# The first mixer's softmax attention, projected first and traced between the other tiles

## The chip, the cores and the metric

The kernel runs on one core of a Trainium2 chip. The metric is the device time of one execution in microseconds (us). Before the change it is 2632.47 us, the median of three runs (2630.48 to 2641.77). All views of the profile below come from one further execution, taken by the hardware profiler.

## The reference

The reference is a stack of four residual layers on 256 context and 256 latent tokens of width 1024; each layer is a mixer followed by a feed-forward network. The change concerns the first mixer only:

```python
h = jnp.concatenate([h_ctx, h_lat], axis=1)                  # 512 tokens x 1024
gq, gk, gv, gog, gz, aq, ak, av = _split(h @ w_in, EVEN_SIZES)
# linear attention, 4 heads: gated recurrence in both directions, norm per head, times silu(gog)
g = _heads(jax.nn.log_sigmoid(logit) / GLA_GATE_TAU, GLA_HEADS)
a_lat = _gated_readout(dirs[0][1] + dirs[1][1], og[:, :, n_ctx:], gla_out_norm)
# softmax attention, 8 query heads on 2 key heads: RMS norm per head, rotary on the latent tokens;
# context queries see the context keys, latent queries see all keys
qa = _rms(aq..., att_q_norm); ka = _rms(ak..., att_k_norm)
b_ctx = _softmax_attend(qa[:, :, :, :n_ctx], ka[:, :, :n_ctx], va[:, :, :n_ctx])
o = jnp.concatenate([a, b], axis=-1)                         # then o @ w_out
```

Everything is computed in float32 accuracy: a projection splits both operands into a high and a low part of type fp32r and adds three products; the attention itself uses plain fp32.

## The kernel before, in words

The text is Python that traces instructions for five engines. A planner then orders them: each instruction has its place in the trace as its priority, an engine takes what is ready and stands first, and a tile waits until one of its `bufs` buffers is free. So a stream that is traced between two pieces of work is offered to the engines there, and a stream that is traced behind them fills gaps. On the chip each engine runs its instructions strictly in the planned order.

The first mixer is `even_mixer`. It first makes the values and the gate's input, `linear_tm` on `ew_tm`, and from these the decay factors `ga` (L545 to L559). Then come 13 projection tiles of 128 output columns, `linear_steps` on `ew_fm` (L591): a 512 KB weight tile is loaded by SP's queue (four `raw` buffers), split by ScalarE and VectorE (L194, L195), and multiplied with all 512 tokens by 24 matmuls in one of the three PSUM banks tagged `pl` (L204 to L206; the first three tiles in two halves). `consume` (L569) takes each result out of PSUM. The order of the tiles is K, Q, K, Q of the linear attention (tiles 0 to 3), the keys and four query tiles of the softmax attention (4 to 8), and four output gates (9 to 12, Silu). For the softmax tiles, `consume` also squares the tile and sums the squares per head and token on TensorE into the bank `ss` (L583).

Two streams follow. `gla` (L610), one for each of two pairs of heads, is the linear attention: seven levels, each with eight fp32 matmuls (sixteen records) in the two `pa` banks, a copy of keys on ScalarE, two masked copies and two products on VectorE; then the products across 128 and 256 tokens; then for each head the product with V, the norm per token (`rstd_rows`, a chain of eleven small VectorE steps), its broadcast by TensorE, and `readout` (L699): VectorE, GpSimd, ScalarE and VectorE in turn write rows 0 to 3 of `M`. `gqa` (L707) is the softmax attention: it makes the norm's factors from `ss`, applies them to the keys, does the rotary products of keys and queries, and then runs 16 units (4 query tiles, 2 key heads, 2 segments of tokens). `attend` (L943) traces the scores and the softmax of a unit (`attend_s`: scores in a `pl` bank, maximum, Exp on ScalarE, reciprocal, scaling) and then the value product of the unit before (`attend_v`: transposes into a `pl` bank, a copy, products into a `pb` bank). After four units `put_hl` (L1013) writes a row of `M` (4 to 7) from the `pb` bank.

`M` takes the two buffers tagged `X` that hold the mixer's input, so it can be allocated only behind the last projection tile. The trace before is: four tiles; then nine tiles, with one step of the two `gla` streams after each; then `M`; then the rest of `gla` and the whole of `gqa` in turn, step by step (L591 to L600). The output projection (`ew_out`) reads the rows of `M` in the order 0 to 7.

Of the kernel before, what the change touches and what calls it, by code (L numbers as in the profile page):

```python
# [8 lines left out]
F32 = mybir.dt.float32  # L9
# [35 lines left out]
def in_turn(streams):  # L45

    streams = list(streams)
    while streams:
        for g in list(streams):
            if next(g, True) is None:  # L50
                yield
            else:
                streams.remove(g)
# [74 lines left out]
class Kern:  # L128
# [396 lines left out]
    def even_mixer(self, X, mix, pre, sc):  # L525
        nc, A = self.nc, self.A
        mm = nc.tensor.matmul
        self.load_masks(mix)
        self.s5_powers(mix, sc)
        V = mix.tile([P, 4, 672], F32, tag="V", name="V0")  # L530

        def put(c, tt, ps):
            nc.scalar.copy(V[:, tt, c * 336:(c + 1) * 336], ps)

        self.linear_tm(A["ew_tm"], X, 4, put, pre=pre)

        zp = self.psum("pa")
        for tt in range(4):
            mm(zp[:32, tt * P:(tt + 1) * P], V[:, tt, 640:672], self.ident, start=True, stop=True)
        z = mix.tile([32, 512], F32, tag="KC", name="z", bufs=2)  # L540
        nc.vector.tensor_copy(z, zp[:32, :])
        wg = mix.tile([32, 2, 256], F32, tag="KC", name="wg", bufs=2)
        nc.sync.dma_start(wg, A["gla_wg"])
        bg = self.gla_bg
        ga = []  # L545
        for t in range(2):
            a = mix.tile([P, 2, 512], F32, tag="g4", name=self.n("gla_a"), bufs=8)
            ab = mix.tile([P, 2, 512], F32, tag="g4", name=self.n("gla_ab"), bufs=8)
            for d in range(2):
                lp = self.psum("pa")  # L550
                mm(lp, wg[:, d, t * P:(t + 1) * P], z, start=True, stop=True)
                nc.scalar.activation(ab[:, d, :], lp, AF.Abs, bias=bg[:, d, t:t + 1])
                nc.vector.tensor_scalar(a[:, d, :], lp, bg[:, d, t:t + 1], 0.0, ALU.add, ALU.min)
            nc.scalar.activation(ab, ab, AF.Exp, scale=-1.0)
            nc.scalar.activation(ab, ab, AF.Ln, bias=1.0)
            nc.vector.tensor_tensor(a, a, ab, ALU.subtract)
            nc.scalar.activation(a, a, AF.Exp, scale=1.0 / 16.0)
            self.dbg(f"gla_a{t}", a)
            ga.append(a)  # L559
        K2 = [mix.tile([P, 2, 512], F32, tag="g4", name=self.n("K2"), bufs=8) for _ in range(2)]  # L560
        Q2 = [mix.tile([P, 2, 512], F32, tag="g4", name=self.n("Q2"), bufs=8) for _ in range(2)]
        qd = [mix.tile([P, 512], F32, tag="qd", name=self.n("qd"), bufs=2) for _ in range(2)]
        sog = mix.tile([P, 4, 512], F32, tag="sog", name="sog")
        qa = mix.tile([P, 4, 512], F32, tag="qa", name="qa")
        kg = mix.tile([P, 512], F32, tag="kg", name="kg")
        ss = self.psum("pb")
        gains = self.even_gains

        def consume(i, ps, *_):  # L569
            if i in (0, 2):  # L570
                nc.scalar.copy(K2[i // 2][:, 0, :], ps)
                nc.vector.tensor_copy(K2[i // 2][:, 1, :], ps)
            elif i in (1, 3):
                t = i // 2
                nc.scalar.mul(qd[t], ps, 0.25)
                for d in range(2):
                    nc.vector.scalar_tensor_tensor(Q2[t][:, d, :], ps, 0.125, ga[t][:, d, :], ALU.mult, ALU.mult)
            elif i < 9:
                sq = self.sm.tile([P, 512], F32, tag="sq", name=self.n("sq"), bufs=2)
                nc.scalar.activation(sq, ps, AF.Square)  # L580
                j = 8 if i == 4 else 2 * (i - 5)
                for tt in range(4):
                    mm(ss[:, 10 * tt + j:10 * tt + j + 2], sq[:, tt * P:(tt + 1) * P], self.hsel, start=True, stop=True)  # L583
                if i == 4:
                    nc.scalar.activation(kg, ps, AF.Identity, scale=gains[:, 1:2])
                else:
                    nc.scalar.activation(qa[:, i - 5, :], ps, AF.Identity, scale=gains[:, 0:1])
            else:
                nc.scalar.activation(sog[:, i - 9, :], ps, AF.Silu)

        tiles = self.linear_steps(A["ew_fm"], X, 512, consume)  # L591
        for _ in range(4):
            next(tiles)
        M = []
        gla = in_turn([self.gla(t, ga[t], K2[t], Q2[t], qd[t], V, sog, gains, M, mix) for t in range(2)])
        for _ in tiles:
            next(gla)
        M += [self.Xp.tile([P, KT, 512], F32R, tag="X", name=self.n("M")) for _ in range(2)]
        for _ in in_turn([gla, self.gqa(qa, kg, ss, V, M, mix)]):
            pass  # L600
        return M

# [104 lines left out]
    def gqa(self, qa, kg, ss, V, M, mix):  # L707
        nc, A = self.nc, self.A
        mm = nc.tensor.matmul
        r = self.sm.tile([P, 4, 10], F32, tag="rs40", name=self.n("rs"), bufs=2)  # L710
        self.rstd_rows(ss[:, :40], 64, 40, r.rearrange("p t h -> p (t h)"))
        rq = self.sm.tile([P, 4, 10], F32, tag="rs40", name=self.n("rq"), bufs=2)
        nc.vector.tensor_scalar(rq, r, 0.125, None, ALU.mult)
        bc = self.psum("pb")
        for h in range(2):
            for tt in range(4):
                mm(bc[64 * h:64 * h + 64, tt * P:(tt + 1) * P], r[:, tt, 8 + h:9 + h].to_broadcast([P, 64]),
                   self.ident, start=True, stop=True, skip_group_check=True)
        nc.vector.tensor_tensor(kg, kg, bc, ALU.mult)
        kz = [mix.tile([P, 512], F32, tag=f"kz{h}", name=self.n("kz")) for h in range(2)]  # L720
        cs = mix.tile([P, 2, 256], F32, tag="rope", name=self.n("rope"))
        nc.sync.dma_start(cs, A["rope0"])

        def rope(x, outs):
            sw = self.psum("pb")
            mm(sw[:, :256], self.perm32, x, start=True, stop=True)
            t = self.sm.tile([P, 512], F32, tag="nt", name=self.n("nt"), bufs=3)
            nc.vector.tensor_tensor(t[:, :256], sw[:, :256], cs[:, 1], ALU.mult)
            nc.vector.tensor_tensor(x, x, cs[:, 0], ALU.mult)
            for o, rs in outs:  # L730
                nc.vector.tensor_tensor(o[rs], x[rs], t[rs, :256], ALU.add)

        for h in range(2):
            rs = slice(64 * h, 64 * h + 64)
            nc.gpsimd.memset(kz[h][64 - 64 * h:128 - 64 * h, :], 0.0)
            nc.gpsimd.tensor_copy(kz[h][rs, :256], kg[rs, :256])
        rope(kg[:, 256:512], [(kz[h][:, 256:512], slice(64 * h, 64 * h + 64)) for h in range(2)])
        for t in range(4):
            rope(qa[:, t, 256:512], [(qa[:, t, 256:512], slice(0, P))])
        yield  # L740

        def units():
            for t in range(4):
                yield from self.pair_units(
                    [(qa[:, t], kz[h], V, slice(512 + 64 * h, 576 + 64 * h),
                      lambda tt, t=t, h=h: rq[:, tt, 2 * t + h:2 * t + h + 1]) for h in range(2)],
                    lambda po, t=t: self.put_hl(po, M, 4 + t))

        yield from self.attend(units(), mix)


# [98 lines left out]
    def hgrn_pair(self, p, al, ac, Kl, Kc, Q2, q, V, sog, gain, mix):  # L850
# [82 lines left out]
        for h in range(2):  # L933
            bc = self.psum(tag)
            for tt in range(2):
                mm(bc[:, tt * P:(tt + 1) * P], r[:, tt * 2 + h:tt * 2 + h + 1].to_broadcast([P, P]), self.ident,
                   start=True, stop=True)
            hd = 2 * p + h
            nc.vector.tensor_tensor(oS[h], oS[h], bc[:, :256], ALU.mult)
            nc.gpsimd.tensor_tensor(sog[:, hd], oS[h], sog[:, hd], ALU.mult)  # L940


    def attend(self, units, mix):  # L943
# [998 lines left out]
def prep(i):  # L1942
# [16 lines left out]
    for p in range(P):  # L1959
# [15 lines left out]
    A["ew_tm"] = np.ascontiguousarray(W[:, tm].reshape(4, 2, P, 2, 336).transpose(3, 0, 2, 1, 4))  # L1975
    aq = np.concatenate([1568 + 64 * h + hd for t in range(4) for h in (t, 4 + t)])
    ak = np.concatenate([2080 + 64 * h + hd for h in range(2)])
    A["ew_fm"] = _tiles(W, np.concatenate([np.arange(256, 384), np.arange(0, 128), np.arange(384, 512), np.arange(128, 256), ak, aq,
                                             np.arange(1024, 1536)]))
    rows = np.concatenate([np.arange(512)] + [512 + 64 * h + np.arange(64) for t in range(4) for h in (t, 4 + t)])  # L1980
    A["ew_out"] = _tiles(i["even_w_out"][0], rows=rows)
    wg = np.zeros((32, 2, 256), f)
# [118 lines left out]
```

## Time and profile before

| | |
|---|---|
| profiled execution | 2632.62 us |
| its span, first to last instruction | 2630.8 us |
| mean granted TensorE clock | 0.954 of full |
| TensorE (PE) matmuls busy | 2420.2 us (92%) |
| VectorE (DVE) busy | 1695.3 us (64%) |
| ScalarE (ACT) busy | 982.1 us (37%) |
| GpSimd (POOL) busy | 503.9 us (19%) |

A busy TensorE is not one at its peak, since its matmuls are pipelined and their ends are modelled. Where matmuls follow each other without a wait, the time from one start to the next is what one of them costs. PEld is TensorE's loading of weights. Times within the trace count from the span's first instruction. The 13 projection tiles run from about 97 to 233 us, and the mixer's last row of `M` is written at 353 us.

### The profile page before, as it was taken

The page shows a single profiled execution, that of the slowest core. Times are in us where ns is not written, and L with a number is a line of the kernel's source. Part 1 is how long each engine was busy: PE and PEld are TensorE (multiplying, and loading weights), DVE is VectorE, ACT ScalarE, POOL GpSimd, SP SyncE. Part 2 cuts the span into 40 slices and gives each one's busy share as a digit, 9 for nine tenths or more (in the row PEclk, how much of TensorE's full clock was granted, in tenths as well). Part 3 has the DMA queues.
Part 4 walks back from the last instruction along what each step waited for, and adds up shares of the span by engine and source line. Part 5 has one row for each costly group of instructions (what it writes and reads, how often), then busy time and mean ns, then how long its engine had stood idle before and what let it go on. Part 6 is the DMA issues. An engine that isn't in the chain of part 4 may idle for free.

```text
span 2630.8 us, 40272 instructions
## 1 busy us (share of the span) xinstructions
PE 2420.2 (92%) x15525; PEld 1974.6 (75%) x15525; DVE 1695.3 (64%) x3417; ACT 982.1 (37%) x1597; POOL 503.9 (19%) x648
## 2 busy tenths in 40 slices
PE   6999998889889988889899999999999999959999
PEld 3567676667678777889699888456787989628999
DVE  4336646998987488975455642665588744485666
ACT  4423424222223253333444443444433223435443
POOL 1810014652720033230100100110100000170000
PEclk9898998999999988999999999999999999989999
DMA  8741032676766234411675532001365533876454
GB/s 270 246 142 41 1 125 74 192 208 189 203 198 194 86 122 142 129 49 65 248 238 182 188 99 88 25 17 35 130 185 183 166 112 97 159 269 231 154 180 152
DMA packets 173294, 382.23 MB, mean 145 GB/s; under 512 B 25296, under 2 KB 71248, under 8 KB 172976
## 3 DMA queue, kind: packets, MB, share of 16 engines
q1 hardware_dynamic: 170096, 372.46, 45.0%
q0 software_dynamic: 3008, 7.21, 1.0%
q8 instruction: 122, 2.00, 0.3%
q14 instruction: 68, 0.56, 0.1%
HBM read 348.94 MB, written 30.67 MB: 144 GB/s over the span
## 4 chain that ended last, share of the span: by engine, by line
PE 46%; DVE 18%; DMA 9%; issue 5%; ACT 3%; POOL 0%; DVEq 0%; SPq 0%; ACTq 0%; POOLq 0%
PE pl L204 11%; PE pl L205 11%; PE pl L206 11%; DVE pm L374 5%; DMA mcol<-ada_t 3%; DVE lo L195 3%; DMA mcol<-mod_t 3%; DMA mrow<-crow 2%; PE pa L76 1%; DVE Wt L1435 1%; PE pa L880 1%; PE pl L963 1%; PE pa L994 1%; PE pm L1267 1%; PE pm L310 1%
## 5 line engine op out<-in xcount | busy, mean ns | idle before, releaser
L194 ACT CAST hi<-raw 128x1024 fp32r<-128x1024 f32 (+4 forms) x393 | 400.2, 1019 | 807.3 <-PE pl L205 610.5
L195 DVE TENSOR_TENSOR lo<-raw,hi 128x1024 fp32r<-128x1024 f32 (+4 forms) x393 | 486.3, 1239 | 315.8 <-ACT hi L194 314.5
L205 PE MATMUL pl<-X,hi 128*128 128x256 f32 (+1 forms) x2032 | 655.3, 324 | 7.4 <-POOL X L469 6.5
L204 PE MATMUL pl<-X,hi 128*128 128x256 f32 (+1 forms) x2032 | 658.9, 326 | 1.9 <-ACT X L466 1.9
L206 PE MATMUL pl<-X,lo 128*128 128x256 f32 (+1 forms) x2032 | 653.9, 323 | 7.2 <-DVE lo L195 7.2
L205 PEld LDWEIGHTS pl<-X,hi 128*128 128x128 f32 x2032 | 397.8, 196 | 45.3 <-issue 9.8
L206 PEld LDWEIGHTS pl<-X,lo 128*128 128x128 f32 x2032 | 397.6, 196 | 42.6 <-DVE lo L195 9.1
L204 PEld LDWEIGHTS pl<-X,hi 128*128 128x128 f32 x2032 | 397.0, 196 | 40.4 <-issue 12.5
L374 DVE SCALAR_TENSOR_TENSOR pm<-mcol,mrow 128x512 f32<-128x512 f32 x384 | 309.4, 806 | 82.7 <-DMA mcol<-ada_t 33.7
L204 PE MATMUL pl<-hh,hi 128*128 128x256 f32 (+1 forms) x1071 | 330.4, 310 | 11.9 <-ACT hh L1673 11.8
L205 PE MATMUL pl<-hl,hi 128*128 128x256 f32 (+1 forms) x1071 | 329.2, 308 | 6.3 <-DVE hl L1674 6.2
L206 PE MATMUL pl<-hh,lo 128*128 128x256 f32 (+1 forms) x1071 | 327.9, 307 | 0.0
L204 PEld LDWEIGHTS pl<-hh,hi 128*128 128x128 f32 x1071 | 204.1, 191 | 33.3 <-ACT hh L1673 13.4
L205 PEld LDWEIGHTS pl<-hl,hi 128*128 128x128 f32 x1071 | 204.8, 191 | 18.9 <-DVE hl L1674 8.4
L206 PEld LDWEIGHTS pl<-hh,lo 128*128 128x128 f32 x1071 | 204.9, 191 | 10.2 <-issue 0.4
L204 PE MATMUL pl<-M,hi 128*128 128x256 f32 (+1 forms) x416 | 124.1, 301 | 0.9 <-ACT M L1016 0.6
L1450 POOL TENSOR_TENSOR Ec<-PGr,bc 128x576 f32<-128x576 f32 x64 | 100.3, 1577 | 127.5 <-PE pb L1458 64.4
L205 PE MATMUL pl<-M,hi 128*128 128x256 f32 (+1 forms) x416 | 121.8, 294 | 0.2 <-DVE M L835 0.2
L206 PE MATMUL pl<-M,lo 128*128 128x256 f32 (+1 forms) x416 | 121.0, 292 | 0.8 <-DVE lo L195 0.8
L1673 ACT CAST hh<-sg 128x512 fp32r<-128x512 f32 (+1 forms) x108 | 55.2, 512 | 175.3 <-DVE sg L1670 110.0
L1687 DVE TENSOR_TENSOR y<-y,pl 128x256 f32<-128x256 f32 (+1 forms) x86 | 45.2, 525 | 107.5 <-PE pl L206 107.0
L469 POOL TENSOR_TENSOR X<-nt,X 128x256 fp32r<-128x256 f32 x48 | 37.7, 785 | 378.5 <-ACT nt L468 378.5
(517 smaller groups left out, 3801.2 us busy)
## 6 DMA issues: line engine op xcount, KB each, us to landing
raw<-f_u SPq DMA_DIRECT2D x88, 512.0 KB, 3.6
raw<-p_u SPq DMA_DIRECT2D x64, 512.0 KB, 3.5
raw<-p_d SPq DMA_DIRECT2D x64, 512.0 KB, 3.6
mraw<-mod_w SPq DMA_DIRECT2D x48, 512.0 KB, 5.2
mcol<-mod_t SPq DMA_DIRECT2D x96, 256.0 KB, 3.1
mcol<-ada_t SPq DMA_DIRECT2D x96, 256.0 KB, 2.9
mraw<-ada_w SPq DMA_DIRECT2D x48, 512.0 KB, 6.8
raw<-ow_fm SPq DMA_DIRECT2D x32, 512.0 KB, 3.3
```

Source lines behind the costliest of these rows:

```text
L76: K.nc.tensor.matmul(self.ps[32 * j:32 * j + 32, :N], K.ones[:rows, :32], self.sq[:rows, :N], start=k < 4, stop=k + 4 >= self.kt, skip_gro ...
L194: nc.scalar.copy(hi, raw)
L195: nc.vector.tensor_tensor(lo, raw, f32(hi), ALU.subtract)
L204: mm(out, w[0][:, kw, wsl], xh, start=first and a == 0, stop=False, skip_group_check=True)
L205: mm(out, w[0][:, kw, wsl], xl, start=False, stop=False, skip_group_check=True)
L206: mm(out, w[1][:, kw, wsl], xh, start=False, stop=last and a == nk - 1, skip_group_check=True)
L310: nc.tensor.matmul(ps[32 * j:32 * j + 32, :], s[:, k, :], raw[:, jj * 512:(jj + 1) * 512], start=k == 0, stop=k == KT - 1, skip_group_chec ...
L374: nc.vector.scalar_tensor_tensor(self.psum("pm"), buf[:, n % 2], 1.0, s[:, v], ALU.mult, ALU.mult, accum_out=(dst if h else part)[:, v, j: ...
L469: nc.gpsimd.tensor_tensor(lo[:, k, a:b], t, f32(hi[:, k, a:b]), ALU.subtract)
L1450: nc.gpsimd.tensor_tensor(Ec[i], ff[i], cs[i], ALU.mult)
L1673: nc.scalar.copy(h, s[:, :N])
L1687: nc.vector.tensor_tensor(y[:, c, a0:b0], y[:, c, a0:b0], ps, ALU.add)
```

## The change

The two softmax inputs come first among the 13 tiles: keys, four query tiles, then K, Q, K, Q, then the gates; the weight array `ew_fm` has its columns in that order. After the first five tiles the preparation of `gqa` is traced, after each of the next four tiles one unit, and after each of the four gates one unit and two steps of `gla`. What is left of both streams is traced in turn behind the tiles, as before. A row of `M` that is finished before `M` can be allocated is copied by ScalarE to a held tile in SBUF (tag `oS`, which the readouts use too), and written to `M` after its allocation.

```diff
@@ even_mixer
         def consume(i, ps, *_):
-            if i in (0, 2):
-                nc.scalar.copy(K2[i // 2][:, 0, :], ps)
...
+            if i < 5:
+                sq = self.sm.tile([P, 512], F32, tag="sq", name=self.n("sq"), bufs=2)
+                nc.scalar.activation(sq, ps, AF.Square)
+                j = 8 if i == 0 else 2 * (i - 1)
...
+            elif i in (5, 7):
+                nc.scalar.copy(K2[i // 2 - 2][:, 0, :], ps)
...
         tiles = self.linear_steps(A["ew_fm"], X, 512, consume)
+        M = []
+        self.held = []
+        for _ in range(5):
+            next(tiles)
+        gqa = self.gqa(qa, kg, ss, V, M, mix)
+        next(gqa)
         for _ in range(4):
             next(tiles)
-        M = []
+            next(gqa)
         gla = in_turn([self.gla(t, ga[t], K2[t], Q2[t], qd[t], V, sog, gains, M, mix) for t in range(2)])
         for _ in tiles:
+            next(gqa)
+            next(gla)
             next(gla)
         M += [self.Xp.tile([P, KT, 512], F32R, tag="X", name=self.n("M")) for _ in range(2)]
-        for _ in in_turn([gla, self.gqa(qa, kg, ss, V, M, mix)]):
+        for put in self.held:
+            put()
+        for _ in in_turn([gla, gqa]):
             pass
@@ gqa
+        keep = self.keep_in(lambda: [mix.tile([P, 512], F32, tag="oS", name=self.n("held"), bufs=4)])
...
-                    lambda po, t=t: self.put_hl(po, M, 4 + t))
+                    lambda po, t=t: self.put_or_hold(po, M, 4 + t, keep))
@@ new
+    def put_or_hold(self, src, M, i, keep):
+        if M:
+            self.put_hl(src, M, i)
+        else:
+            src = keep(src)
+            self.held.append(lambda: self.put_hl(src, M, i))
+    def keep_in(self, room):
+        rows = []
+        def keep(src):
+            if not rows:
+                rows.extend(room())
+            at = rows.pop(0)
+            self.nc.scalar.copy(at, src)
+            return at
+        return keep
@@ prep
-    A["ew_fm"] = _tiles(W, np.concatenate([np.arange(256, 384), np.arange(0, 128), np.arange(384, 512), np.arange(128, 256), ak, aq,
-                                             np.arange(1024, 1536)]))
+    A["ew_fm"] = _tiles(W, np.concatenate([ak, aq, np.arange(256, 384), np.arange(0, 128), np.arange(384, 512),
+                                             np.arange(128, 256), np.arange(1024, 1536)]))
```

## Rows read from the trace of the kernel before

**Rows 1.** The page: shares of the span in the chain that ended last.

```profile
PE 46%; DVE 18%; DMA 9%; issue 5%; ACT 3%; POOL 0%; DVEq 0%; SPq 0%; ACTq 0%; POOLq 0%
```

**Rows 2.** Stages: stretch, length, busy (x instructions) per engine, clock, DMA share, GB/s.

```profile
211.00:236.00 25.00, 25.00 (x153) 20.58 (x153) 13.75 (x20) 8.32 (x12) 0.00 (x0) 1.00 0.24 81
236.00:247.00 11.00, 9.04 (x51) 6.60 (x50) 10.96 (x27) 1.18 (x2) 1.34 (x2) 1.00 0.02 9
247.00:261.00 14.00, 13.14 (x44) 8.25 (x44) 8.72 (x26) 6.50 (x15) 0.00 (x0) 0.51 0.01 2
261.00:285.00 24.00, 24.00 (x124) 15.75 (x123) 15.16 (x41) 8.38 (x21) 0.00 (x0) 1.00 0.00 1
285.00:325.00 40.00, 39.11 (x237) 28.66 (x236) 24.08 (x79) 18.43 (x41) 5.31 (x4) 1.00 0.00 1
325.00:352.80 27.80, 24.50 (x115) 14.09 (x114) 14.97 (x45) 11.88 (x28) 0.00 (x0) 1.00 0.00 0
```

**Rows 3.** Timeline of TensorE, last projection tiles: start, duration, instruction, count.

```profile
216.81 1.71 PE L640 MATMUL pa<-Q,KC 64*128 64x128 f32 x16
224.13 1.71 PE L640 MATMUL pa<-Q,KC 64*128 64x128 f32 x16
...
233.09 1.58 PE L717 MATMUL pb<-pack_sb,rs 128*64 128x128 f32 x16
```

**Rows 4.** Timeline of ScalarE behind the last tile; in brackets the idle time before.

```profile
246.44 0.62 ACT L636 COPY KC<-K 128x512 f32<-128x512 f32 x1 [9.47 <-DVE K L646]
247.07 1.28 ACT L969 ACT_TABLE_LOAD   x1
248.37 0.56 ACT L969 ACTIVATE Pm<-pl,mx,rq 128x256 f32<-128x256 f32 x1
```

**Rows 5.** Groups of TensorE's instructions by form, 236 to 353 us: count, busy, mean ns.

```profile
L994 PE MATMUL pb<-PT,V 128*64 128x256 f32 x96 | 26.3, 401 | 1.8 <-ACT PT L989 1.6 <-DVE PT L991 0.2
L963 PE MATMUL pl<-kz,qa 128*128 128x512 f32 x32 | 18.4, 660 | 0.0
L985 PE MATMUL pl<-pack_sb,Pm 128*128 128x128 f32 x96 | 16.6, 293 | 1.7 <-DVE Pm L972 1.5 <-ACT Pm L969 0.2
...
L963 PE MATMUL pl<-kz,qa 128*128 128x256 f32 x32 | 10.3, 432 | 0.4 <-ACT Pm L969 0.4
```

**Rows 6.** Timeline of TensorE, softmax units in the tail.

```profile
321.11 1.09 PE L985 MATMUL pl<-pack_sb,Pm 128*128 128x128 f32 x8
322.04 1.02 PE L963 MATMUL pl<-kz,qa 128*128 128x512 f32 x2
...
340.63 1.13 PE L963 MATMUL pl<-kz,qa 128*128 128x512 f32 x2
341.68 1.94 PE L994 MATMUL pb<-PT,V 128*64 128x256 f32 x8
343.55 1.13 PE L963 MATMUL pl<-kz,qa 128*128 128x512 f32 x2
```

**Rows 7.** Timeline of VectorE: one level's masked copies; one softmax's first and last step.

```profile
218.91 1.36 DVE L642 COPY_PREDICATED S<-masks,pa 128x512 f32<-128x512 int32 x2
...
341.79 0.69 DVE L965 TENSOR_REDUCE mx<-pl 128x1 f32<-128x512 f32 x1
...
343.89 0.49 DVE L972 TENSOR_SCALAR Pm<-Pm,smx 128x512 f32<-128x512 f32 x1
```

**Rows 8.** Timeline of TensorE and VectorE: readouts of both pairs of heads.

```profile
293.59 0.39 PE L687 MATMUL pa<-S,V 128*128 128x128 f32 x2
303.54 1.92 DVE L705 TENSOR_TENSOR M<-oS,M 128x512 fp32r<-128x512 f32 x2 [1.22 <-ACT M L704]
308.70 0.39 PE L687 MATMUL pa<-S,V 128*128 128x128 f32 x2
318.55 2.05 PE L695 MATMUL pa<-pack_sb,rs 128*128 128x128 f32 x16
324.20 0.68 DVE L705 TENSOR_TENSOR M<-oS,M 128x512 fp32r<-128x512 f32 x1
```

More of the change, by code (lines that the diff above doesn't have):

```diff
@@ L569, in consume @@
         def consume(i, ps, *_):
-            if i in (0, 2):
-                nc.scalar.copy(K2[i // 2][:, 0, :], ps)
-                nc.vector.tensor_copy(K2[i // 2][:, 1, :], ps)
-            elif i in (1, 3):
-                t = i // 2
+            if i < 5:
+                sq = self.sm.tile([P, 512], F32, tag="sq", name=self.n("sq"), bufs=2)
+                nc.scalar.activation(sq, ps, AF.Square)
+                j = 8 if i == 0 else 2 * (i - 1)
+                for tt in range(4):
+                    mm(ss[:, 10 * tt + j:10 * tt + j + 2], sq[:, tt * P:(tt + 1) * P], self.hsel, start=True, stop=True)
+                if i == 0:
+                    nc.scalar.activation(kg, ps, AF.Identity, scale=gains[:, 1:2])
+                else:
+                    nc.scalar.activation(qa[:, i - 1, :], ps, AF.Identity, scale=gains[:, 0:1])
+            elif i in (5, 7):
+                nc.scalar.copy(K2[i // 2 - 2][:, 0, :], ps)
+                nc.vector.tensor_copy(K2[i // 2 - 2][:, 1, :], ps)
+            elif i in (6, 8):
+                t = i // 2 - 3
                 nc.scalar.mul(qd[t], ps, 0.25)
@@ L577, in consume @@
                     nc.vector.scalar_tensor_tensor(Q2[t][:, d, :], ps, 0.125, ga[t][:, d, :], ALU.mult, ALU.mult)
[L578 to L587, printed above, removed]
             else:
@@ L940, in hgrn_pair @@
             nc.gpsimd.tensor_tensor(sog[:, hd], oS[h], sog[:, hd], ALU.mult)
+    def put_or_hold(self, src, M, i, keep):
+        if M:
+            self.put_hl(src, M, i)
+        else:
+            src = keep(src)
[9 more added lines that the diff above has]
+        return keep
     def attend(self, units, mix):
```

## The prediction

> **What bounds the kernel now.** I read the page's chain of waits first, then the first mixer alone, stage by stage. TensorE leads the chain [rows 1], but that is an average over the whole span, and the change touches one mixer of four. The table of that mixer's stages [rows 2] is what to read. From 211 to 236 us, the last projection tiles, TensorE is busy all 25 us at full clock, while VectorE has 13.75 and ScalarE 8.32: TensorE sets this stage. The last tiles follow each other every 7.32 us, of which 1.71 are the sixteen matmul records of one linear-attention level [rows 3], so a tile's own 24 matmuls take 5.61, or 0.234 each. From 236 to 352.8 us (116.8 us, here called the tail) no projection is left: softmax units, linear-attention levels and readouts depend on each other, and TensorE waits. The worst part is its beginning. Between 236 and 247 TensorE has 9.04 busy of 11; between 247 and 261 it is granted 0.51 of its clock, which is the 1.2 GHz level [rows 2]. Before it fell, the matmuls waited for VectorE, which was busy 10.96 of 11 us there with rotary products and level updates, and ScalarE stood idle for 9.47 us until an update of K released it [rows 4].
>
> The measure is the profiled execution: 2632.62 us, of which the span is 2630.8, and 1.8 lie around it. The median of the three runs is 2632.47, so no correction is needed.
>
> **The change part by part.** It moves work within this mixer. It adds one ScalarE copy and some table loads, and removes nothing.
>
> *Work that goes into the projection stage.* At the end of the tiles the softmax stream has taken nine steps instead of none: its preparation, the scores of units 0 to 7, and the value products of units 0 to 6. The linear attention has taken eight steps, one fewer than now. Counts come from [rows 5], where each fp32 matmul has two records: of 16 units' 32 + 32 score records half move, of 96 transposes and 96 value products 40 each (four context units of 4, three latent units of 8), and the ten rotary records. Prices are from start to start [rows 6]. One latent query tile's scores take 1.05 us: 8 of them, 8.4. Context ones have half the columns, so by estimate 0.525: 8, 4.2. Eight transposes take 0.93: 40, 4.65. Eight value products take 1.87: 40, 9.35. The ten rotary records have the context scores' width: 2.6. Together 29.2 us, less one level of 1.71: 27.5 us. In the projection stage TensorE has no free time, so that stage gets 27.5 us longer, and the tail's work gets 27.5 us less. By itself this is zero. What counts is which waits go and which come.
>
> *The start of the tail, which goes.* The reciprocal roots, the rotary products and the masked keys now lie beside projection tiles. Lost there today: 14.0 x (1 - 0.51) = 6.9 us of clock, and 1.96 + 0.86 = 2.8 of idle time [rows 2]. Together 9.7. That is the upper end, since some matmuls there would have waited at full clock too; the lower end is the 2.8 of idle time. I take 9.7, for the tail will now open with scores and levels whose inputs are ready. Late next is the ordinary give and take of unit and level, already in 261 to 285 us, where TensorE counts as busy throughout.
>
> *Waits that come into the projection stage.* Projection tiles, scores and transposed probabilities share the three PSUM banks "pl". A latent unit's two score tiles take two, the tile just finished holds the third until it is copied out. A matmul that waits for a bank has the next tile's matmuls behind it on TensorE's queue, and the whole stage waits for them. A score bank comes free only after maximum, scaling and exponential; from the maximum to the normalised row it is 2.6 us today [rows 7]. There are eight such handovers. At best none waits: the unit's own matmuls, the value products of the unit before and, in the last four tiles, two levels (3.4 us) stand in front. At worst each waits the whole 2.6: 21 us. The nearest row is the stage today, which has a level between tiles and no idle time [rows 2, 3], so I stay near the lower end: 0.3 each, 2.5 us.
>
> *Load on the other engines.* In each of the last four tiles VectorE gets a second level (1.36 for its two masked copies [rows 7], by estimate as much again for its two products: 2.7) and a unit (per query tile 0.69 + 0.49 [rows 7] and two small steps, by estimate 1.5 with a copy of 0.7 beside: at most 3.7) on top of its 13.75 of 25, that is about 4 per tile: some 10 us. TensorE then has 5.6 + 3.4 + a unit of about 3.3 = 12.3. It stays the longer one. GpSimd's mask copies find it idle (0.00 of 25 in [rows 2]). The rotary table is one small transfer on SP's queue, the 13 weight tiles keep their size, only their order in memory changes; nothing is gained or lost on that queue. The held copy and its later cast from SBUF lie on ScalarE: some 0.6 us, hidden by the same TensorE work, 0.6 if not.
>
> *Table loads.* The four gates (Silu) now stand between units (Exp), so by the code ScalarE changes its table eight times where now one change for the gates and one for the units do: six more. One load takes 1.28 us [rows 4], so 7.7 us more on an engine that is busy 8.32 of 25. I count them at zero; the cover is TensorE's 12.3 us per tile.
>
> The Trainium skill speaks against this edit. Its page "ScalarE: Activation LUTs", section "What ACT_TABLE_LOAD costs", gives about 2.66 us for a change of set, 1283 ns of load and 1380 ns of drain, and asks to group functions by set. Here the load's 1283 ns agree, but the copy before it runs up to the load, and the exponential starts 1.30 us after the load began [rows 4]; no drain is to be seen. By the page's figure the six would be 16 us of ScalarE, still less than its free time in the stage.
>
> *The end of the tail, which gets worse.* Today the linear attention's readouts lie in 285 to 325 us with units around them (TensorE busy 39.11 of 40), and the tail ends with units, 3.3 us idle in 325 to 352.8 [rows 2]. After the change eight units are left for eight levels, and the readouts come behind both in trace order: they end the mixer. From the last value product of a pair of heads to its last row for the output projection: 293.98 to 305.46 us, 11.5, for the first pair; 309.09 to 324.88, 15.8, for the second [rows 8]. Beside that lies the last unit's 0.93 + 1.87, the sums (by estimate 1) and the broadcasts (2.05 [rows 8]), and three output tiles' products with the first pair's rows (18 at 0.117, 2.1): 8.0 in all. Uncovered: 3.5 to 7.8; I take 6. And the two pairs share the two "pa" banks with less beside them: 0 to 5, I take 1. So 7 come where 3.3 go: 3.7 worse.
>
> **Sum:** 2632.6 - 9.7 + 2.5 + 3.7 = 2629.1; I say 2629.
>
> **The rivals.**
> *A: all waits find cover.* Then the projection stage adds none, the readouts slide in between units, and the tail's end costs no more than today: 2632.6 - 9.7 = 2622.9; and as levels and units are now eight to eight, the two streams fill each other's gaps in the second half too. TensorE's records in 325 to 352.8 leave 3.3 idle, and short waits hidden in the records of 261 to 325 I estimate at 5. That gives 2615. For it: the planner reorders well (the key-norm broadcasts, traced behind all tiles, stand among the levels before the tail [rows 3]). Against: the readout's chain is serial.
> *B: the banks decide.* Each of the eight handovers waits for the chain of 2.6 us, and the last four for a Silu load and an Exp load too (8 x 1.28 = 10.2, no longer hidden, since they delay the release of the same banks): 31 us instead of 2.5. That is 2629 + 28.5 = 2657; with half the waits hidden, 2643, and 2650 between. It decides from the point where two score banks and one uncopied projection tile leave no bank for the next matmul for longer than levels and value products last. Against it: a gate tile's bank is read by one ScalarE instruction, and levels use other banks.
> *C: the table loads alone land on the path:* 6 x 1.28 = 7.7, 2637. This is what the skill's advice to group by set would make of it.
> *D: the change doesn't do what it says.* The planner, not the trace, sets each engine's order; it may put the units behind the tiles as now. Then 2632.
>
> **How the numbers follow.** Forecast 0.48, A 0.23, B 0.17, C 0.07, D 0.05. About 0.5%, 13.2 us, is what a measurement can tell from no change: 2619.3 to 2645.6. Faster is A: 0.23. Slower is B: 0.17. The rest is the same: 0.60. The forecast's own range is 2621 to 2638. The range for 8 in 10 takes in most of A (to 2612) and the milder half of B (to 2647).
>
> **What would show it.** Right: the last gate after 250 us; the projection stage some 27 to 30 us longer and the tail 30 or more shorter; no half-clock stretch at the tail's start; the last rows of M written by the readout and not by a unit; eight table loads in place of two. Wrong: TensorE idle between tiles for a score bank (B); ScalarE's load named as what a score or a tile waits for (C); units all behind the last gate (D); the readouts finished before the last units and a tail under 80 us (A). A new half-clock stretch at the readouts or at the start of the output projection would put up to 7 us on top.

## The result, and the profile after

The changed kernel takes 2656.16 us (median; 2655.11 to 2657.31), the kernel before 2632.22 us beside it: ratio 1.0092, 95% interval 1.0071 to 1.0113, so 24 us slower. 2629 had been forecast, with a range to 2647. The span of the profiled execution is 2655.4 us, 24.6 more than before, and the last row of the first mixer's result M is written at 380.4 us [378.00 + 2.41, in the view of the mixer's end below]; before it was 353.0. That is 27.4 later, so the whole loss is made inside this mixer, and 2.8 us of it come back behind.

The shares of the chain, which answer to [rows 1], hide it:

```profile
PE 47%; DVE 17%; DMA 8%; issue 4%; ACT 3%; POOL 0%; DVEq 0%; SPq 0%; ACTq 0%; POOLq 0%
```

The stages of the mixer after the change, as in [rows 2]: stretch, length, busy (x instructions) of TensorE, its weight loads, VectorE, ScalarE, GpSimd, clock, DMA share, GB/s.

```profile
138.00:165.00 27.00, 17.94 (x51) 5.54 (x48) 1.92 (x4) 4.51 (x8) 4.60 (x9) 0.57 0.53 179
165.00:189.00 24.00, 24.00 (x99) 19.75 (x98) 4.82 (x14) 4.63 (x7) 0.00 (x0) 0.77 0.14 44
189.00:240.00 51.00, 45.22 (x211) 32.89 (x210) 28.03 (x66) 16.06 (x31) 0.79 (x2) 1.00 0.13 42
240.00:286.00 46.00, 44.06 (x232) 32.10 (x230) 27.14 (x55) 24.76 (x39) 0.00 (x0) 0.96 0.10 35
286.00:330.00 44.00, 43.15 (x241) 27.85 (x239) 35.15 (x86) 19.78 (x44) 0.00 (x0) 1.00 0.04 13
330.00:345.00 15.00, 15.00 (x82) 10.55 (x80) 9.61 (x26) 5.70 (x14) 0.00 (x0) 1.00 0.00 1
345.00:367.00 22.00, 18.68 (x132) 15.83 (x131) 6.85 (x19) 6.67 (x13) 2.49 (x2) 1.00 0.00 1
367.00:381.00 14.00, 9.71 (x63) 8.79 (x62) 5.49 (x15) 2.41 (x4) 2.54 (x2) 0.87 0.00 1
```

The kernel before in the first two of these stretches, which the prediction did not read:

```profile
138.00:165.00 27.00, 26.75 (x136) 15.24 (x136) 6.80 (x10) 6.95 (x10) 4.13 (x7) 1.00 0.67 225
165.00:189.00 24.00, 23.96 (x124) 19.21 (x125) 12.74 (x15) 7.27 (x11) 0.00 (x0) 0.93 0.14 45
```

Three places stand out. From 138 to 165 us TensorE runs 51 instructions where it ran 136, at a mean clock of 0.57. From 189 to 240 it is idle for 5.8 us. And in the last two stretches it is idle for 3.3 + 4.3 us, while in [rows 2] the mixer's last 27.8 us had 3.3 in all. What it waits for (time, times, longest): the first four lines are from 165 to 290 us, the last three from 290 to 385:

```profile
PE pl L204 <- DVE K L582: 2.6, 1, 2.6
PE pl L1017 <- DVE K L582: 2.0, 1, 2.0
PE pl L1017 <- ACT Pm L1001: 1.5, 2, 1.3
PE pb L1026 <- ACT PT L1021: 0.7, 1, 0.7
...
PE pa L705 <- DVE rs L399: 5.0, 2, 2.8
PE pl L205 <- DVE M L715: 1.4, 3, 1.0
PE pl L204 <- ACT M L714: 1.1, 1, 1.1
```

The end of the mixer, as in [rows 8], TensorE and VectorE; the idle time before each is in brackets:

```profile
358.72 2.02 PE L705 MATMUL pa<-pack_sb,rs 128*128 128x128 f32 x16 [2.84 <-DVE rs L399]
...
373.53 3.37 PE L705 MATMUL pa<-pack_sb,rs 128*128 128x128 f32 x16 [2.13 <-DVE rs L399]
378.02 0.62 PE L204 MATMUL pl<-M,hi 128*128 128x256 f32 x3 [1.12 <-ACT M L714]
...
378.00 2.41 DVE L715 TENSOR_TENSOR M<-oS,M 128x512 fp32r<-128x512 f32 x2 [0.32 <-ACT M L714]
```

The first place is explained by two timelines. ScalarE, where the reader of [rows 4] looks for the idle time in front of an instruction:

```profile
159.91 0.58 ACT L313 COPY modcp<-pm 128x512 f32<-128x512 f32 x1 [21.02 <-PE pm L310]
160.39 0.60 ACT L572 ACTIVATE sq<-pl 128x512 f32<-128x512 f32 x1
160.88 0.69 ACT L577 ACTIVATE kg<-pl,pack_sb 128x512 f32<-128x512 f32 x1
162.52 0.60 ACT L572 ACTIVATE sq<-pl 128x512 f32<-128x512 f32 x1 [0.95 <-PE pm L317]
```

And TensorE beside it. The modulation (L310) is a product with a large weight matrix, loaded piece by piece while the tiles run; its matmuls each wait for a transfer of weights:

```profile
139.48 1.05 PE L310 MATMUL pm<-mraw,s_cc 128*32 128x512 f32 x4 [0.58 <-DMA mraw<-mod_w]
142.73 1.92 PE L310 MATMUL pm<-mraw,s_cc 128*32 128x512 f32 x4 [2.19 <-DMA mraw<-mod_w]
...
157.94 1.92 PE L310 MATMUL pm<-mraw,s_cc 128*32 128x512 f32 x4 [1.00 <-DMA mraw<-mod_w]
160.54 1.88 PE L317 MATMUL pm<-pack_sb,modcp 128*128 128x8 f32 x8 [0.68 <-ACT modcp L313]
```

The first projection tile's Square (L572) stands in ScalarE's queue behind the copy of the modulation's sums (`modcp`, L313). That copy needs all of L310's matmuls, which run at the pace of the weights. Until then nothing empties the three "pl" banks with the first three tiles, and no fourth tile can begin. Both instructions take a buffer of the same two (tag `sq`). Before, the first four tiles were the linear attention's, which need no Square; their copies out ran at 118, 131, 140 and 150 us:

```profile
118.13 0.59 ACT L571 COPY K<-pl 128x512 f32<-128x512 f32 x1
130.59 0.59 ACT L575 ACTIVATE qd<-pl 128x512 f32<-128x512 f32 x1
139.94 0.58 ACT L571 COPY K<-pl 128x512 f32<-128x512 f32 x1
150.27 0.59 ACT L575 ACTIVATE qd<-pl 128x512 f32<-128x512 f32 x1
```

### The profile page after: what moved, and what is told of

Read it like the earlier page. It is cut to its first block, busy times and chain, and to the rows that moved or that the text cites. A ratio compares the mean times of both kernels' runs of the same rounds, so it can differ in the third digit from the quotient of the medians.

```text
span 2655.4 us, 40265 instructions
## 1 busy us (share of the span) xinstructions
PE 2429.3 (91%) x15525; PEld 1982.3 (75%) x15525; DVE 1694.8 (64%) x3417; ACT 989.4 (37%) x1604; POOL 503.4 (19%) x648
## 4 chain that ended last, share of the span: by engine, by line
PE 47%; DVE 17%; DMA 8%; issue 4%; ACT 3%; POOL 0%; DVEq 0%; SPq 0%; ACTq 0%; POOLq 0%
PE pl L204 11%; PE pl L205 11%; PE pl L206 11%; DVE pm L374 5%; DVE lo L195 3%; DMA mcol<-ada_t 3%; DMA mcol<-mod_t 3%; PE pa L76 1%; DVE Wt L1467 1%; PE pa L891 1%; PE pl L995 1%; PE pa L1026 1%; PE pm L1299 1%; PE pb L1292 1%; DVE Wt L1468 1%
```

## The experiments

Theory 1: the Squares behind the modulation's copy cost most of the 24 us. Theory 2: the units between tiles do, by waits for banks (rival B of the prediction). Times are compared by their ratio to the kernel before, run on the same chip; one per cent is 26.3 us.

**The Squares' own buffers.** In the changed kernel, and in the kernel before:

```diff
-                sq = self.sm.tile([P, 512], F32, tag="sq", name=self.n("sq"), bufs=2)
+                sq = mix.tile([P, 512], F32, tag="PT", name=self.n("sq"), bufs=2)
```

> The changed kernel, with the Square of the first five projection tiles written to a pair of buffers that is free at that time (that of the transposed softmax rows) and no longer to the pair that the copy of the modulation's sums also takes. Theory 1 (the Squares stand behind that copy, the copy waits for the modulation's weights, and so three tiles hold the three banks from about 128 to 160 us): the first Square comes before 135 us, the idle time of 21 us in front of the copy is not in front of any Square, and the time falls by 15 to 19 us, to 2637 to 2641 us. Rival a (TensorE waits there for the modulation's weights in any case): within 3 us of 2656 us, the first Square early or not. Rival b (all 24 us are made between 189 and 286 us, where units and gates share the banks): also within 3 us of 2656 us.

Measured: 2637.22 us, ratio 1.0013 (1.0001 to 1.0025), so 20.8 us of the 24.2 are gone. ScalarE, and the waits of TensorE from 100 to 165 us:

```profile
116.83 0.58 ACT L572 ACTIVATE sq<-pl 128x512 f32<-128x512 f32 x1
...
128.90 0.59 ACT L572 ACTIVATE sq<-pl 128x512 f32<-128x512 f32 x1
...
163.28 0.58 ACT L313 COPY modcp<-pm 128x512 f32<-128x512 f32 x1 [2.99 <-PE pm L310]
...
PE pm L310 <- DMA mraw<-mod_w: 1.1, 2, 0.7
```

The copy comes at 163.3, no earlier than in the changed kernel, and now nothing waits behind it; TensorE's waits for the weights are 1.1 us, where the changed kernel has 9.3 between 118 and 176 us, because projection matmuls fill them. Rival a falls: the transfers were late in both, only their cover had gone.

> The kernel before, with the same edit: its Squares (fifth to ninth tile) get the pair of buffers of the transposed softmax rows. Theory 1: before had four tiles that need no Square, so little stood behind the copy; the fifth tile's Square comes some us before 160 and the time falls by 0 to 4 us, to 2628 to 2632 us. Rival (a general gain from another pair of buffers, whatever the order of the tiles): it falls as much as the changed kernel does by this edit, to about 2615 us.

Measured: 2632.13 us, ratio 0.9995 (0.9982 to 1.0009): nothing. The buffers matter only where Squares come first.

**The two halves of the change alone.** Order only: the units and their preparation are taken out from between the tiles.

```diff
-        for _ in range(5):
-            next(tiles)
-        gqa = self.gqa(qa, kg, ss, V, M, mix)
-        next(gqa)
-        for _ in range(4):
-            next(tiles)
-            next(gqa)
+        for _ in range(9):
+            next(tiles)
...
         for _ in tiles:
-            next(gqa)
             next(gla)
             next(gla)
...
-        for _ in in_turn([gla, gqa]):
+        for _ in in_turn([gla, self.gqa(qa, kg, ss, V, M, mix)]):
```

> The changed order of the tiles alone: softmax attention projected first, but its preparation and all its units traced behind the tiles as in the kernel before; the linear attention gives two steps per gate. Theory 1 (the stall at 138 to 176 us belongs to the order of the tiles): it is all here, 15 to 19 us above the kernel before, 2647 to 2651 us, with the first Square near 160 us and a half clock of over 30 us around it. Theory 2 (the loss belongs to the units between the tiles): 2630 to 2635 us.

Measured: 2645.08 us, ratio 1.0039 (1.0027 to 1.0051). The stall is whole:

```profile
155.10 0.58 ACT L313 COPY modcp<-pm 128x512 f32<-128x512 f32 x1 [21.95 <-PE pm L310]
155.58 0.60 ACT L572 ACTIVATE sq<-pl 128x512 f32<-128x512 f32 x1
```

The time is only 10.3 us above before, less than the 15 to 19 expected. With the Squares' own buffers the same order tells why:

> The changed order of the tiles with all units behind them, as the run of the order alone (2645 us), and the Squares' own pair of buffers. Theory 1: the whole of the 12 us of that run is the stall behind the modulation's copy, so 2631 to 2635 us, like the kernel before. Rival (half of it belongs to something else in that order, as the keys of the linear attention that come later): 2638 to 2642 us.

Measured: 2624.44 us, ratio 0.9963 (0.9948 to 0.9978). The stall is worth 20 us here too (1.0039 - 0.9963), and the order without it is 9.7 us better than before. Theory 1 had it equal to before, and its rival above it; that gain is a miss of mine (below). Three lines of its trace: one stretch of its tail, its last gate's copy, and its last row of M (before, the last two start at 232.3 and 352.3):

```profile
240.00:286.00 46.00, 43.96 (x214) 28.42 (x215) 32.47 (x87) 18.79 (x43) 0.00 (x0) 0.89 0.00 1
...
224.38 0.59 ACT L589 ACTIVATE sog<-pl 128x512 f32<-128x512 f32 x1
...
347.01 0.69 DVE L1043 TENSOR_TENSOR M<-pb,M 128x512 fp32r<-128x512 f32 x1 [3.02 <-ACT M L1042]
```

Units between the gates only, with the tiles in the order of before (rows of M are held as in the change):

```diff
+        for _ in range(5):
+            next(tiles)
+            next(gla)
+        gqa = self.gqa(qa, kg, ss, V, M, mix)
+        next(gqa)
         for _ in tiles:
+            next(gqa)
             next(gla)
...
-        for _ in in_turn([gla, self.gqa(qa, kg, ss, V, M, mix)]):
+        for _ in in_turn([gla, gqa]):
```

> The units between the gates alone: the tiles in the order of the kernel before (linear attention's inputs first), the preparation of softmax attention behind the ninth tile, one unit before each of the four gates, results held as in the change. Fewer units come forward (four, not eight). Theory 1 with the forecast's prices: no stall at 138 to 176 us, half of the tail's gain, 2625 to 2632 us. Theory 2 (units between tiles cost more in waits for banks than the tail gives back): 2636 to 2645 us.

Measured: 2627.26 us, ratio 0.9975 (0.9966 to 0.9985), 6.6 us faster. Four units between gates pay, so theory 2 fails for these; the 14 us by which the change lies above the order alone (1.0092 - 1.0039) are followed further down.

**What is left: banks, tables, readouts.** The three that follow start from the changed kernel with the Squares' own buffers (ratio 1.0013).

```diff
-        yield from self.attend(units(), mix)
+        yield from self.attend(units(), mix, "pb")
...
-            pt = self.psum("pl")
+            pt = self.psum(bank)
```

> The changed kernel with the Squares' own pair of buffers (2637 us), and the transposes of the units of this mixer in the pair of banks that collects their results, no longer in the three banks of the projection tiles. Theory 2 (what is left over the kernel before is mostly waits for those three banks): the waits of TensorE for VectorE's K copies (2.0 and 2.4 us) and for a gate's copy go, and the time falls by 4 to 8 us, to 2629 to 2633 us. Rival (those waits are VectorE's and ScalarE's own lateness: the copies stand behind preparation and softmax in their queues): within 2 us of 2637 us.

Measured: 2633.93 us, ratio 1.0004 (0.9989 to 1.0020). The interval overlaps that of 1.0013, so this run alone does not decide. In its trace the 2.0 us wait of a transpose for `K` is gone, that of the next tile stays at 2.3, and M is complete 5.1 us earlier (354.6 against 359.7).

```diff
-                nc.scalar.activation(sog[:, i - 9, :], ps, AF.Silu)
+                nc.scalar.activation(sog[:, i - 9, :], ps, AF.Identity)
```

> The changed kernel with the Squares' own pair of buffers (2637 us), and the four gates copied without the Silu, so that the six more table loads and the switches between Silu and Exp fall away; the output lacks the Silu. The forecast's step (six loads cost ScalarE 7.7 us that stay hidden): within 2 us of 2637 us. Rival C (the loads lie on the path): 2629 to 2630 us.

This kernel leaves the Silu out of the result. Measured: 2634.71 us, ratio 1.0014 (0.9999 to 1.0028): by ratio the same as with the loads. Rival C's 7.7 us (0.0029) would lie below that interval, and falls. A smaller cost is not excluded: the intervals reach 3 to 4 us to each side, and in the trace without the loads TensorE's waits in the units for an exponential and for a gate's copy (1.5 and 0.6 us) are down to 0.2 and nothing, and the last gate's copy comes 4.3 us earlier (257.8 against 262.1). In the changed kernel each gate has its pair of loads, as in [rows 4]:

```profile
240.26 1.28 ACT L589 ACT_TABLE_LOAD   x1
241.56 0.60 ACT L589 ACTIVATE sog<-pl 128x512 f32<-128x512 f32 x1
242.17 1.28 ACT L1001 ACT_TABLE_LOAD   x1
```

The Silu starts 1.30 us after its load began, and the next load 0.01 after the Silu ends. The drain of 1380 ns that the Trainium skill's page "ScalarE: Activation LUTs", section "What ACT_TABLE_LOAD costs", adds to each change is not to be seen here either.

```diff
-        for _ in in_turn([gla, gqa]):
-            pass
+        for _ in gqa:
+            next(gla, None)
+            next(gla, None)
+        for _ in gla:
+            pass
```

> The changed kernel with the Squares' own pair of buffers (2637 us), and behind the gates two steps of the linear attention to each unit, so that its readouts come before the last three units and not at the very end. Theory 3 (the readouts at the end cost what their waits show: TensorE idle 5.0 us for the norm's factors, 1.7 us for the first rows of the result, and part of a half clock behind them): 2629 to 2632 us. Rival (the last units, with nothing left to trace between them, give back what the readouts leave): within 2 us of 2637 us.

Measured: 2622.71 us, ratio 0.9963 (0.9949 to 0.9977), 13 us better than with the readouts at the end, beyond the range of theory 3. Without this edit (the own buffers alone) the two stretches at the end read

```profile
330.00:345.00 15.00, 12.13 (x71) 10.59 (x70) 5.88 (x16) 4.17 (x7) 2.52 (x2) 0.77 0.01 2
345.00:367.00 22.00, 18.10 (x104) 17.04 (x104) 5.48 (x15) 2.41 (x4) 2.53 (x2) 0.69 0.26 86
```

and with it

```profile
330.00:345.00 15.00, 14.38 (x97) 11.38 (x97) 7.26 (x21) 4.95 (x9) 2.52 (x2) 1.00 0.00 1
345.00:367.00 22.00, 22.00 (x153) 19.40 (x151) 9.92 (x9) 5.02 (x9) 4.99 (x3) 1.00 0.83 302
```

The stretches do not hold the same work, since with the edit the second is output projection already. Over the whole tail, from the last gate's copy to the last row of M (262.1 to 359.7 without the edit, 260.1 to 345.0 with it), TensorE's idle time falls from 7.7 to 2.5 us. The mean clocks of 0.77 and 0.69 mean that 15 x 0.46 + 22 x 0.62 = 20.5 us were at the 1.2 GHz level, part of them behind the mixer's end; that is gone. M is complete at 345.0 instead of 359.7, by a unit:

```profile
344.28 0.69 DVE L1052 TENSOR_TENSOR M<-pb,M 128x512 fp32r<-128x512 f32 x1 [0.24 <-ACT M L1051]
```

The same edit with the shared buffers left as the change has them:

> The changed kernel with the shared pair of buffers left as it is, and only the order of the tail edited: two steps of the linear attention to each unit behind the gates. If the stall behind the modulation's copy and the readouts at the end are two separate causes, the tail's edit is worth here what it was worth beside the other buffer (14 us): 2656 less 14, so 2639 to 2645 us. Rival (the readouts only came late because the stall, or its removal, shifted the stage): under 5 us, 2651 us or more.

Measured: 2642.34 us, ratio 1.0038 (1.0023 to 1.0052), 14.2 us better than the change. The two causes are separate and add: 20.8 and 13.1 with the one mended first, 19.7 and 14.2 with the other. With the tail's order mended the change lies where the order alone does (1.0038 and 1.0039), so the 14 us that its units seemed to add belong to the order of its tail.

**Towards a faster kernel.** Own buffers, no units between keys and queries, one unit and two levels before each gate:

```diff
-        for _ in range(5):
+        for _ in range(9):
             next(tiles)
         gqa = self.gqa(qa, kg, ss, V, M, mix)
         next(gqa)
-        for _ in range(4):
-            next(tiles)
-            next(gqa)
...
         for _ in tiles:
             next(gqa)
             next(gla)
             next(gla)
```

> The changed order of the tiles with the Squares' own buffers, no unit between the keys' and queries' tiles, and one unit with two linear-attention steps in front of each of the four gates; behind them unit and step in turn. Set between the run with all units behind the tiles (2624 us) and the one with eight units among the tiles (2623 us with the tail in order). Theory 4 (units between the gates pay, as in the kernel before, where they were worth 6 us; those between keys and queries pay for waits for VectorE): 2616 to 2621 us. Rival (units among tiles give nothing once the stall and the tail are mended): 2622 to 2627 us.

Measured: 2616.44 us, ratio 0.9945 (0.9928 to 0.9962), 4.7 us better by ratio than the order alone and than eight units; the intervals of 0.9963 and 0.9945 overlap, so the sign is likely and not settled. Its waits from 165 to 290 us hold no wait for `K` any more:

```profile
PE pb L1023 <- ACT PT L1018: 0.7, 1, 0.7
PE pl L1014 <- ACT sog L589: 0.3, 1, 0.3
PE pl L204 <- ACT sog L589: 0.3, 1, 0.3
PE pb L734 <- DVE nt L736: 0.3, 1, 0.3
```

All three edits together, with eight units among the tiles:

> All three edits of the changed kernel together: the Squares' own buffers, two linear-attention steps to each unit in the tail, and the units' transposes in the pair of banks of their results. If the banks were worth the 3 us that they seemed to be: 2617 to 2621 us. If they are worth nothing: 2622 to 2624 us.

Measured: 2616.49 us, ratio 0.9941 (0.9921 to 0.9962), 15.5 us faster than before and 39.7 faster than the change. Against 0.9963 without the bank edit the intervals overlap again; both runs of that edit point to 2 to 6 us.

## Why the prediction was wrong, step by step

*The work moved into the projection stage* came out as forecast in its sum, by two misses that cancel. With the stall mended the last gate's copy comes at 262.1 us, before at 232.3: 29.8 later, in the range of 27 to 30 named as the sign. But from 97 us to that copy TensorE is busy 24.0 us longer than before (156.7 against 132.7) and idle 5.8 us longer (8.4 against 2.6), where 27.5 and 2.5 had been forecast. And the step said "by itself this is zero", and that failed. The prediction read the trace from 211 us on and took the new order of the tiles as one of memory alone. It did not follow the first tiles' instructions through ScalarE's queue and the buffers they take. What came in its place is the stall from 138 to 176 us, worth 20 us in three pairs of runs (the change and its own-buffer version, the order alone, the mended tail). What the experiments show is that the buffer decides. That the planner puts the Squares behind the copy because the copy took its buffer first in trace order is read from the two lines of code and from the order of the queue, in which the Squares go ahead once they have other buffers.

*The start of the tail* was right: the half-clock stretch at 247 to 261 us [rows 2] is gone, and the stretch from 286 to 330 us is granted 1.00. In the changed order with all units behind the tiles a low stretch is still there (0.89 in 240 to 286 us), so it is the units among the tiles that remove it. The tail as a whole, from the last gate's copy to the last row of M, went from 120.7 us (232.3 to 353.0) to 95.6 (284.8 to 380.4). That is 25.1 shorter, where 30 or more had been named as the sign; the missing part is in the next step.

*The end of the tail* was right in its mechanism and mis-sized. The readouts do end the mixer, and they leave TensorE idle for 7.6 us between 345 and 381 (3.3 + 4.3), close to the 7 of the forecast. But the term of +3.7 is too small: the edit of the tail's order gives back 13 to 14 us, and in the traces it makes the tail 10.6 us shorter in the changed kernel (95.6 to 85.0) and 12.7 in the one with its own buffers (97.6 to 84.9). The forecast set only the 3.3 us idle of today's end against it. A tail ordered with the readouts inside is better than that: its last 15 us hold 0.6 us of idle time. And the clock was left out, in spite of the sentence at the prediction's end: a mean clock of 0.87 in 367 to 381, which is 14 x 0.26 = 3.6 us at the low level, in the change, and 20.5 us of it with the buffers mended. How the 13 us divide between clock and idle time was not measured alone, and the edit reorders the whole tail behind the gates, not only its end.

*The waits in the projection stage* were 2.5 in the forecast. The trace after has 7.8 us of named waits between 165 and 290 (6.8 in the four above, and 1.0 in three small ones), and the greater part isn't the chain of maximum and exponential that was priced. It is 4.6 us for VectorE's copy of K. VectorE of the change shows why:

```profile
192.09 0.42 DVE L739 TENSOR_TENSOR nt<-pb,rope 128x256 f32<-128x256 f32 x1 [0.93 <-POOL kz L747]
...
196.96 0.42 DVE L740 TENSOR_TENSOR qa<-qa,rope 128x256 f32<-128x256 f32 x1
197.30 0.68 DVE L582 COPY K<-pl 128x512 f32<-128x512 f32 x1
```

ScalarE had copied its half of this tile at 192.69; VectorE's half came at 197.30, behind the rotary products, and TensorE stood idle for 2.57 us in front of the next tile's matmul. The prediction had counted VectorE's sum of work (it stays below TensorE's) and not its order. Of rival B, the place was right and the size a quarter, 7.8 of 31, and more than half of that for this other reason.

*The table loads* were counted rightly, eight. That they are free is not settled: no cost shows in the time, and the traces leave room for up to 4 us (above).

*The sum.* The forecast had the projection stage 30.0 us longer (27.5 + 2.5) and the tail 33.5 shorter (27.5 + 9.7 - 3.7). In the traces the stage is 52.5 longer (232.3 to 284.8) and the tail 25.1 shorter. So the error at the mixer's end is 22.5 us in the stage, which the stall makes up (the own-buffer version has its last gate 22.7 us earlier), and 8.4 in the tail. With the two causes mended the change is 9.7 us faster than before by ratio, between the forecast (-3.5) and rival A (-17.6). This does not confirm the forecast's gain: the changed order with its own buffers and all units behind the tiles has the same ratio, 0.9963. Against that kernel the eight units among the tiles lengthen the stage by 35.7 us (last gate at 224.4 and 260.1) and shorten the tail by 38.4 (123.3 to 84.9), and no gain of theirs shows in the time.

Open is why the changed order, freed of the stall and with all units behind it, is 9.7 us faster than the order of before, where I expected nothing. In the traces 5.3 us of this lie in the mixer (M complete at 347.7 instead of 353.0). The last gate's copy comes 7.9 us earlier, with two levels of the linear attention fewer in front of it (105 records of their products against 73, about 3.4 us), and the tail is only 2.6 us longer. The runs do not show where the rest comes from.

## What to carry to other kernels

When tiles are reordered, follow the first of them to the instruction that empties its bank, and ask what stands before that on its engine and which buffers it shares: a pair of buffers shared with something that waits for a transfer turns a harmless copy into a gate for the whole stage. When two streams fill each other's gaps, let the one with the long serial ending finish first; here that was worth 13 to 14 us. An engine whose total is small can still be late; read the order of its queue where another engine waits for its one short copy.

## What the runs showed of the hardware

In the changed kernel TensorE fell to the 1.2 GHz level although no wait from 138 to 165 us was longer than 2.2 us. It was busy 17.94 of these 27 us, 13.5 of them with L310's matmuls of the form 128x32; four of these took 1.05 us at 139.48 us and 1.92 from 142.73 us on, and the mean granted clock was 0.57. In the own-buffer kernel the same matmuls, mixed with projection matmuls, left 26.26 of 27 busy at 1.00. So the stall has two parts: matmuls that could not begin, and projection matmuls behind it that ran slower at first (0.77 in 165 to 189 us; 0.43 us from one start to the next at 171 us, 0.23 at 177). That the slower L310 cost time is not shown, since each of them waited for its weights in any case.
